# Split weights at five offsets modulo 256 bytes, split activations at another

## The chip, the cores and the metric

The kernel runs on one core of one Trainium2 chip. The metric is the device time of the program in microseconds; before the change it is 2554.64 us, the median of three runs (2552.96 to 2555.19).

## The reference, cut to what matters

Two transformer blocks run one after the other on 256 tokens of width 1024, all in float32. The first has two layers with a feed-forward network, a token mixer and a second feed-forward network, over 256 latent tokens and 256 context tokens. The second has three branches (dilated attention, a short convolution, attention on a memory), gates, and a mixture of 32 experts.

```python
def _swiglu(h, w1, w3, w2):
    return (jax.nn.silu(h @ w1) * (h @ w3)) @ w2
...
    for l in range(DEPTH):
        lat = lat + 0.5 * ml[2] * _swiglu(_modulate(lat, ...), *ffn1)
        cx = cx + 0.5 * mc[2] * _swiglu(_modulate(cx, ...), *ffn1)
        ...
        out_lat, _, _ = _token_mixer(_modulate(lat, ...), *mix_w, s_f, s_b)
        lat = lat + ml[5] * out_lat
        ...
# second block
        merged = (gates[:, :, 0] * (o_attn @ w_proj_attn[l])
                  + gates[:, :, 1] * (z_conv @ w_proj_conv[l])
                  + gates[:, :, 2] * (o_mem @ w_proj_mem[l]))
        x = x + merged @ w_out[l]
        x = x + _hierarchical_moe(h2, ...)   # top 2 of 8 experts of the best of 4 groups
```

The change touches no arithmetic. What matters is that nearly every product before the experts is a float32 matrix product with a weight matrix that is used once.

## The kernel before

All weights of the two blocks but the experts come as units of 128 partitions by 2048 floats (1 MB), in the order in which they are used. `Stream` brings them in: `issue` starts the transfer of a unit into one of three slots `raw`, and `pump` splits each half of it (1024 columns) in two. ScalarE writes the rounded part `wh` in the format fp32r (line 313), VectorE the rest `wl = raw - wh` (line 314). There are five pairs of such tiles (`NSPLIT`), each in a pool of its own (`pst0` to `pst4`), used in turn. A split pair is 8 weight tiles of 128 by 128, or 2 of 128 by 512.

The activations are split the same way: `xh`, `xl` hold the normalised input of a layer (8 tiles of 128 features by 512 tokens), `hh`, `hl` the hidden values of the feed-forward networks, `om` and `mgh`, `mgl` smaller ones of the second block. `mm3` (lines 402 to 404) makes a product of three matmuls: `wl` with `xh`, `wh` with `xl`, `wh` with `xh`. The weights are the stationary operand, which a separate weight load puts in place, the activations the moving one. `wide` (lines 971 to 973) does it the other way round, with the weights moving, 512 columns at a time. With latent and context tokens together a moving operand has 512 columns, with one of them 256. In the profile `p` is the output of the first two feed-forward products, `po` that of output projections, `pz` that of input projections.

Other matrix products (the scan of the mixer, attention, the experts) take plain float32 operands. The experts' weights come as 192 units of 1 MB (`moe_issue`) into whatever tile is free: `moe` in the three raw slots, `ring`, `moex`, `moeom`, `moemgl`, `moexh`, `moexl` and `X`. Expert weights are the moving operand there (lines 1729 and 1757).

The transfers of weights are all issued on the SyncE queue, in the order of the units. The order of the work on each engine follows from the code's order; the `Threads` object interleaves the mixer's scan with the matmuls by a clock of its own.

Tiles are placed by pools that grow from the left or from the right end of a partition's memory. Two fillers set the offsets: `edge` (line 425, 8 floats) on the left ahead of `xh` and `xl`, and `rim` (line 477, 56 floats) on the right after the raw slots, ahead of all pools that follow. `t2` tiles, the scan's `M`, `Q`, `AB` and other left-hand tiles lie after `edge` as well. In the built program the addresses of the main tiles in a partition are, in bytes and modulo 256:

| tile | address before | modulo 256 | address after | modulo 256 |
|---|---|---|---|---|
| X | 16512 | 128 | 16512 | 128 |
| xh, xl (later moexh, moexl) | 33024, 49408 | 0 | 32992, 49376 | 224 |
| hh, hl | 130816, 147200 | 0 | the same | 0 |
| wh, wl of pair 4 | 163584, 167680 | 0 | the same | 0 |
| wh, wl of pair 3 | 171776, 175872 | 0 | 171808, 175904 | 32 |
| wh, wl of pair 2 | 179968, 184064 | 0 | 180064, 184160 | 96 |
| wh, wl of pair 1 | 188160, 192256 | 0 | 188320, 192416 | 160 |
| wh, wl of pair 0 | 196352, 200448 | 0 | 196576, 200672 | 224 |
| raw slots (later moe) | 204544, 212736, 220928 | 0 | 204768, 212960, 221152 | 224 |
| t2 tiles (G, sT, ffa and others) | 76704 and on | 160 | 76672 and on | 128 |
| junk, sc of the modulation | 114208, 95264 | 32 | 114176, 95232 | 0 |
| mgh, mgl, moeom, moemgl | 89440, 154976 | 96 | 89408, 154944 | 64 |
| ring, moex | 97632, 163168 and on | 96 | 97600, 163136 and on | 64 |
| ht, xg of the experts | 188160, 196352 | 0 | 188384, 196576 | 224 |

Every slice that a matmul reads of `wh`, `wl`, `xh`, `xl`, `hh`, `hl`, `mgh` or `mgl` starts a multiple of 512 bytes into its tile, so it has its tile's offset modulo 256.

Of the kernel before, what the change touches and what calls it, by code (L numbers as in the profile page):

```python
# [9 lines left out]
F = mybir.dt.float32  # L10
# [163 lines left out]
R2_QN, R2_KN, R2_QM, R2_KM, R2_B, NR2 = 0, 64, 128, 256, 384, 420  # L174
SUB = 32
OWN = 7
EDGE = (8, 56)


def level_masks():  # L180
# [194 lines left out]
class Kernel:  # L375
# [34 lines left out]
    def run(self):  # L410
        tc, nc, a, es = self.tc, self.nc, self.a, self.es
        self.pc = es.enter_context(tc.tile_pool(name="pc", bufs=1))
        self.pw = es.enter_context(tc.tile_pool(name="pw", bufs=1))
        self.prw, _ = self.pool("prw", "right")
        self.pst = [self.pool("pst%d" % i, "right") for i in range(NSPLIT)]
        self.pf, self.pf_end = self.pool("pf", "right")
        self.pm, self.pm_end = self.pool("pm")
        self.ps = es.enter_context(tc.tile_pool(name="ps", bufs=1, space=PSUM))
        pc = self.pc
        self.S = Stream(self, self.units, a["ws"])  # L420
        self.th = Threads()
        self.X = pc.tile([128, 8, 512], F, name="X")
        self.eps = pc.tile([128, 1], F, name="eps")
        self.lbc = pc.tile([128, 2, 2, 4], F, name="lbc")
        self.edge = pc.tile([128, EDGE[0]], F, name="edge")
        self.operands()
        self.cols = pc.tile([128, NCOL], F, name="cols")
        self.cst = pc.tile([128, NCST], F, name="cst")
        load = nc.sync.dma_start
        load(self.cols, a["cols"])  # L430
        load(self.cst, a["cst"])
        self.post = self.pm.tile([128, 512], F, name="post", tag="AB", bufs=4)[:, :256 + 4 * (T // 64)]
        load(self.post, a["post"])
        load(self.X[:, :, 0:256], a["xin"][:, :, 0:256])
        load(self.X[:, :, 256:512], a["xin"][:, :, 256:512])
        for u in range(NADA):
            load(self.ada_raw[u], a["ws"][u])
            if u in (1, 3):
                self.S.issue(NADA + (u + 1) // 2)
        self.S.issue(NADA + NRAW)  # L440
        self.msk = self.pm.tile([128, 5, 128], I32, name="msk")
        nc.sync.dma_start(self.msk, a["msk"])
        self.ident = self.cst[:, CST_ID:CST_ID + 128]
        self.ones = self.cst[:, CST_ONE:CST_ONE + 128]
        self.sel = self.cst[:, CST_SEL:CST_SEL + 2]
        nc.gpsimd.memset(self.eps, EPS)
        self.scp = pc.tile([128, 8, 36], F, name="scp", tag="scp")[:, :, 0:32]
        nc.gpsimd.memset(self.scp, 0.0)
        nc.scalar.activation(self.scp[:, :, 0:2], self.col("c", "p (a b) -> p a b", b=2), AF.Silu)
        self.lower_bounds()  # L450
        self.spread()
        self.mods = [pc.tile([128, 72, 2], F, name=f"mods{l}") for l in range(2)]
        self.stat_tiles()
        self.AB = {}
        self.first()
        self.second()
        self.moe()
# [16 lines left out]
    def operands(self):  # L474

        self.ada_tiles()
        self.prw.tile([128, EDGE[1]], F, name="rim")

    def ada_tiles(self):

# [1373 lines left out]
```

## Time and profile before

| what | value |
|---|---|
| median of three runs | 2554.64 us |
| profiled execution | 2556.33 us, span 2554.5 us |
| TensorE busy | 2399.6 us, 94% of the span, 14237 matmuls |
| weight loads busy | 1921.3 us, 75% |
| VectorE busy | 1401.8 us, 55% |
| ScalarE busy | 933.7 us, 37% |
| GpSimd busy | 96.4 us, 4% |
| mean granted clock of TensorE | 0.959 |
| read from memory | 510.01 MB, 200 GB/s over the span |

Matmuls are pipelined: each is shown from its start to a modelled end, and overlaps the next. Their rate is read from the distance of starts, or from how many fit in a stretch. A weight load overlaps the matmul before it. In the rows, `out<-in` gives the tiles' names without buffer numbers; of a matmul the moving operand and the stationary one are both inputs.

### The profile page before, as it was taken

To read this page: it belongs to the slowest core of one execution; us is meant where nothing else is said; L and a number is where in the kernel's file an instruction comes from. 1 tells how busy PE (TensorE), PEld (TensorE's weight loads), DVE (VectorE), ACT (ScalarE), POOL (GpSimd) and SP (SyncE) were. 2 spreads that over 40 slices of the span, in tenths; PEclk is the share of its full clock that TensorE was granted. 3 is DMA by queue.
4 is the path that set the end of the run, shared out by engine and by line. 5 is a ranking of instruction groups with operands and counts; after the bars stand their busy time and mean duration, and the time that the engine had idled before them with its cause. 6 is when DMAs were issued, how large, how long until landed. Compare 5 with 4: busy or idle time off the path is not lost.

```text
span 2554.5 us, 34811 instructions
## 1 busy us (share of the span) xinstructions
PE 2399.6 (94%) x14237; PEld 1921.3 (75%) x14237; DVE 1401.8 (55%) x2458; ACT 933.7 (37%) x1481; POOL 96.4 (4%) x125
## 2 busy tenths in 40 slices
PE   7999999999999999999999989999999999776766
PEld 6888888888988888988888879999888984221211
DVE  5777745776787634887534686655776651000000
ACT  5322234676432223422224576545645641000000
POOL 2000001000100001000001010001000000000000
PEclk8999999999999999999999999999999999878877
DMA  7455532112365422455322324555543779999998
GB/s 294 172 191 198 187 126 95 67 50 100 134 229 198 165 99 112 152 210 192 138 89 97 128 73 147 182 182 182 194 144 121 275 285 407 417 415 417 414 417 343
DMA packets 91399, 513.40 MB, mean 201 GB/s; under 512 B 8208, under 2 KB 31264, under 8 KB 32096
## 3 DMA queue, kind: packets, MB, share of 16 engines
q1 hardware_dynamic: 90096, 508.29, 52.4%
q8 instruction: 114, 1.87, 0.3%
q0 software_dynamic: 560, 1.87, 0.2%
q10 hardware_dynamic: 576, 0.94, 0.1%
q14 instruction: 53, 0.43, 0.1%
HBM read 510.01 MB, written 1.05 MB: 200 GB/s over the span
## 4 chain that ended last, share of the span: by engine, by line
PE 44%; DMA 11%; DVE 2%; ACT 1%; SPq 1%; issue 1%; POOL 0%; DVEq 0%; ACTq 0%
PE p L402 5%; PE p L404 5%; PE p L403 5%; DMA ring<-wm 4%; PE po L403 3%; PE po L402 3%; PE po L404 3%; PE pz L402 3%; PE pz L403 3%; PE pz L404 3%; DMA moe<-wm 2%; DMA moex<-wm 2%; DMA moexh<-wm 2%; PE my L1757 2%; PE wide L973 1%; PE wide L971 1%
## 5 line engine op out<-in xcount | busy, mean ns | idle before, releaser
L314 DVE TENSOR_TENSOR wl<-raw,wh 128x1024 fp32r<-128x1024 f32 x428 | 526.7, 1232 | 339.6 <-ACT wh L313 336.1
L313 ACT ACTIVATE wh<-raw 128x1024 fp32r<-128x1024 f32 x428 | 451.6, 1057 | 604.0 <-PE po L404 247.8
L402 PE MATMUL p<-xh,wl 128*128 128x512 f32 (+1 forms) x1608 | 554.5, 347 | 2.0 <-ACT xh L612 2.0
L403 PE MATMUL p<-xl,wh 128*128 128x512 f32 (+1 forms) x1608 | 555.5, 346 | 0.4 <-DVE xl L613 0.4
L404 PE MATMUL p<-xh,wh 128*128 128x512 f32 (+1 forms) x1608 | 555.0, 346 | 0.0
L402 PEld LDWEIGHTS p<-xh,wl 128*128 128x128 f32 x1608 | 303.8, 190 | 41.0 <-ACT xh L612 2.9
L403 PEld LDWEIGHTS p<-xl,wh 128*128 128x128 f32 x1608 | 304.9, 190 | 38.6 <-DVE xl L613 1.1
L404 PEld LDWEIGHTS p<-xh,wh 128*128 128x128 f32 x1608 | 305.0, 190 | 37.0
L512 DVE SCALAR_TENSOR_TENSOR junk<-raw,sc 128x1024 f32<-128x1024 f32 x256 | 304.1, 1234 | 19.1 <-DMA raw<-ws 13.4
L403 PE MATMUL po<-hl,wh 128*128 128x512 f32 (+1 forms) x767 | 266.5, 348 | 0.1
L402 PE MATMUL po<-hh,wl 128*128 128x512 f32 (+1 forms) x767 | 266.4, 348 | 0.0
L404 PE MATMUL po<-hh,wh 128*128 128x512 f32 (+1 forms) x767 | 266.2, 347 | 0.0
L402 PE MATMUL pz<-xh,wl 128*128 128x256 f32 (+1 forms) x672 | 223.7, 333 | 0.0
L403 PE MATMUL pz<-xl,wh 128*128 128x256 f32 (+1 forms) x672 | 211.9, 315 | 0.0
L404 PE MATMUL pz<-xh,wh 128*128 128x256 f32 (+1 forms) x672 | 211.7, 315 | 0.0
L403 PEld LDWEIGHTS po<-hl,wh 128*128 128x128 f32 x767 | 145.2, 189 | 19.1 <-DVE hl L730 0.7
L404 PEld LDWEIGHTS po<-hh,wh 128*128 128x128 f32 x767 | 145.2, 189 | 18.1
L402 PEld LDWEIGHTS po<-hh,wl 128*128 128x128 f32 x767 | 145.0, 189 | 18.3
L727 ACT ACTIVATE ffa<-p 128x512 f32<-128x512 f32 (+1 forms) x88 | 47.9, 544 | 249.2 <-PE p L404 249.2
L402 PEld LDWEIGHTS pz<-xh,wl 128*128 128x128 f32 x672 | 128.4, 191 | 11.6 <-issue 6.2
L404 PEld LDWEIGHTS pz<-xh,wh 128*128 128x128 f32 x672 | 128.3, 191 | 7.5 <-issue 0.2
L403 PEld LDWEIGHTS pz<-xl,wh 128*128 128x128 f32 x672 | 128.6, 191 | 5.7 <-issue 0.5
(424 smaller groups left out, 2908.8 us busy)
## 6 DMA issues: line engine op xcount, KB each, us to landing
raw<-ws SPq DMA_DIRECT2D x279, 1024.0 KB, 4.8
ring<-wm SPq DMA_DIRECT2D x66, 1024.0 KB, 15.4
moe<-wm SPq DMA_DIRECT2D x27, 1024.0 KB, 13.1
moex<-wm SPq DMA_DIRECT2D x27, 1024.0 KB, 16.9
moexh<-wm SPq DMA_DIRECT2D x18, 1024.0 KB, 19.7
moexl<-wm SPq DMA_DIRECT2D x18, 1024.0 KB, 19.7
X<-wm SPq DMA_DIRECT2D x18, 1024.0 KB, 20.2
moeom<-wm SPq DMA_DIRECT2D x9, 1024.0 KB, 20.1
```

The source lines that it names most:

```text
L313: k.nc.scalar.activation(wh, raw, AF.Copy)
L314: k.nc.vector.tensor_sub(wl, raw, wh.bitcast(F))
L402: mm(out, wl, xh, start=start, stop=False, **kw)
L403: mm(out, wh, xl, start=False, stop=False, **kw)
L404: mm(out, wh, xh, start=False, stop=stop, **kw)
L512: v.scalar_tensor_tensor(junk, raw[:, i * 1024:i * 1024 + 1024], 1.0, self.sc[:, p], op0=OP.mult, op1=OP.mult, accum_out=m[:, t + i, p:p + 1])
L727: nc.scalar.activation(t, p1, AF.Silu)
L971: mm(q[n], self.xl[:, kc, ts], wh, start=kc == 0, stop=False)
L973: mm(q[n], self.xh[:, kc, ts], wh, start=False, stop=kc == 7)
L1757: mm(py[32 * j:32 * j + 32, :], hT[:, c * 128 + 32 * j:c * 128 + 32 * j + 32], w[:, c % 2 * 4 + j], start=c == 0, stop=c == 3, skip_group_ ...
```

## The change

The filler `edge` goes, and the filler `rim` goes from the raw slots' pool to the pools of the split weights: 16, 16, 16 and 8 floats (64, 64, 64 and 32 bytes) in `pst0` to `pst3`, none in `pst4`. The sum of the fillers on the right is 56 floats as before, so `hh` and `hl` stay where they were. All engines issue the same instructions in the same order with the same waits; the addresses are as in the table above.

```diff
-EDGE = (8, 56)
+STEP = (16, 16, 16, 8, 0)
...
         self.lbc = pc.tile([128, 2, 2, 4], F, name="lbc")
-        self.edge = pc.tile([128, EDGE[0]], F, name="edge")
         self.operands()
...
         self.ada_tiles()
-        self.prw.tile([128, EDGE[1]], F, name="rim")
+        for (p, _), n in zip(self.pst, STEP):
+            if n > 0:
+                p.tile([128, n], F, name="rim")
```

## Rows read from the trace of the kernel before

**Rows 1.** Busy time by stage: us of each engine, granted clock, DMA share, GB/s
```profile
core 0: us, PE busy (x) PEld busy (x) DVE busy (x) ACT busy (x) POOL busy (x), PEclk, DMA share, GB/s
0.00:60.00 60.00, 46.73 (x342) 37.21 (x346) 31.16 (x68) 32.03 (x59) 13.85 (x20) 0.83 0.75 293
60.00:2110.00 2050.00, 2027.83 (x11583) 1774.34 (x11575) 1342.65 (x2329) 876.88 (x1371) 82.53 (x105) 1.00 0.42 154
2110.00:2555.00 445.00, 325.08 (x2324) 109.73 (x2316) 28.03 (x62) 24.80 (x51) 0.00 (x0) 0.81 1.00 405
```

**Rows 2.** Groups by line and form: count, busy us, mean ns, idle before; 512-column matmuls
```profile
L402 PE MATMUL p<-xh,wl 128*128 128x512 f32 x944 | 367.3, 389 | 0.0
...
L402 PE MATMUL po<-hh,wl 128*128 128x512 f32 x465 | 180.9, 389 | 0.0
...
L972 PE MATMUL wide<-wl,xh 128*128 128x512 f32 x224 | 87.4, 390 | 0.0
...
L402 PE MATMUL pz<-xh,wl 128*128 128x512 f32 x184 | 79.3, 431 | 0.0
...
L402 PE MATMUL po<-xh,wl 128*128 128x512 f32 x40 | 15.6, 389 | 0.0
```

**Rows 3.** Busy time by stage, of line 402 alone
```profile
60.00:2110.00 2050.00, 1104.05 (x3241) 613.80 (x3241) 1.00 0.42 154
```

**Rows 4.** Busy time by stage, a stretch of 512-column and one of 256-column matmuls
```profile
700.00:1000.00 300.00, 300.00 (x1325) 248.43 (x1324) 187.21 (x276) 81.56 (x99) 0.00 (x0) 1.00 0.44 162
1036.00:1058.00 22.00, 22.00 (x184) 21.95 (x183) 17.93 (x37) 11.57 (x20) 0.00 (x0) 1.00 0.18 67
```

**Rows 5.** Timeline of TensorE (start us, duration us), five matmuls left out at each dots
```profile
1059.01 0.40 PE L402 MATMUL p<-xh,wl 128*128 128x512 f32 x1
...
1060.40 0.39 PE L402 MATMUL p<-xh,wl 128*128 128x512 f32 x1
...
1061.76 0.39 PE L402 MATMUL p<-xh,wl 128*128 128x512 f32 x1
```

**Rows 6.** Timeline of TensorE, matmuls on mgh and mgl (2 and 17 left out)
```profile
2064.11 0.28 PE L404 MATMUL po<-mgh,wh 128*128 128x256 f32 x1
...
2064.47 0.29 PE L404 MATMUL po<-mgh,wh 128*128 128x256 f32 x1
...
2066.63 0.29 PE L404 MATMUL po<-mgh,wh 128*128 128x256 f32 x1
```

**Rows 7.** Plain fp32 matmuls by line and by tile: duration ns min/median/max, starts
```profile
L1757 PE MATMUL my<-ring,mhT x336: 379/379/634, 2139.4 to 2544.6; 128*32 128x256 f32 x168
...
L1757 PE MATMUL my<-moe,mhT x128: 379/379/634, 2356.3 to 2469.9; 128*32 128x256 f32 x128
...
L1664 PE MATMUL gat<-G,ht x128: 379/379/796, 2101.7 to 2407.7; 128*128 128x256 f32 x128
...
L1766 PE MATMUL xt<-mys,sT x128: 379/379/797, 2134.9 to 2546.4; 128*128 128x256 f32 x128
```

**Rows 8.** VectorE and ScalarE by line and by tile: duration ns min/median/max
```profile
L314 DVE TENSOR_TENSOR wl<-raw,wh x428: 1207/1225/1874, 23.0 to 2074.3; 128x1024 fp32r<-128x1024 f32 x143
...
L512 DVE SCALAR_TENSOR_TENSOR junk<-raw,sc x256: 1215/1222/1760, 59.2 to 1228.8; 128x1024 f32<-128x1024 f32 x128
...
L313 ACT ACTIVATE wh<-raw x428: 1040/1060/1087, 21.9 to 2073.2; 128x1024 fp32r<-128x1024 f32 x143
...
L729 ACT ACTIVATE hh<-ffa x88: 399/615/636, 76.4 to 1769.3; 128x512 fp32r<-128x512 f32 x66, 128x256 fp32r<-128x256 f32 x22
...
L1517 ACT ACTIVATE mgh<-X x8: 398/404/420, 2041.5 to 2066.5; 128x256 fp32r<-128x256 f32 x8
```

**Rows 9.** Last line of the tile views of raw, moe and ring: issue to landing
```profile
DMA to landing us min/median/max: 4.6/4.8/18.4
...
DMA to landing us min/median/max: 4.8/13.1/20.2
...
DMA to landing us min/median/max: 4.9/15.4/21.5
```

## The prediction

> **What bounds the kernel now.** I read the table of stages first [rows 1]. The span of 2554.5 us has three parts. In the first 60 us TensorE waits for loads. From 60 to 2110 us TensorE is busy for 2027.83 of 2050 us at a granted clock of 1.00 (the 2.4 GHz level), VectorE for 1342.65 and ScalarE for 876.88, the DMA engines for 0.42. From 2110 us on the DMA engines are busy all the time (1.00, 405 GB/s) and TensorE waits for expert weights. So the matmul rate sets the middle, the transfer rate sets the tail, and the splitting engines set next to nothing: the time in which TensorE stands still in the middle is 2050 - 2028 = 22 us.
>
> Then the groups by line and form, and the starts of single matmuls. Nearly all of the middle is triples of split matmuls: 3241 starts on line 402 there [rows 3], as many on 403 and 404, and the 224 wide triples of lines 971 to 973. The 512-column ones are 944 + 465 + 184 + 40 + 224 = 1857 triples [rows 2], 5571 matmuls; the rest of line 402, 3241 - 1633 = 1608 triples, 4824 matmuls, has 256 columns (1633 is the 1857 without the 224 wide ones). Together 10,395. In a stretch with nothing but 512-column ones, 1325 of them fill 300.00 us, and in one with nothing but 256-column ones 184 fill 22.00 us [rows 4], which is 226.4 and 119.6 ns each, with a matmul at each edge counted too often. The starts give it without that error: 1060.40 to 1061.76 us is six spacings of 226.7 ns [rows 5], and the 256-column ones come at 120.0 ns (below). The two differ by 106.7 ns for 256 columns, 0.417 ns a column, which is the 2.4 GHz level; on top of its columns each matmul costs the same 13.3 ns at both widths. TensorE already runs back to back, so an effect of addresses has to show in this 13.3 ns, in the column rate, or not at all.
>
> **What the change does.** It adds and removes no instruction, no wait and no transfer, and the order on every engine stays as it is. It moves bytes. Split activations (xh, xl) go from offset 0 modulo 256 to 224; the five pairs of split weights from 0 to 224, 160, 96, 32 and 0; the raw weight slots from 0 to 224; the hidden activations (hh, hl) stay at 0; nearly all other tiles on the left side go 32 bytes down. So every term is a duration at one offset against the same duration at another, and the trace of before holds tiles at several offsets already.
>
> **Moving operand of a split matmul, off the 256-byte grid.** The output projection of the second block streams mgh and mgl, which lie at offset 96, over weights at 0. The 21 spacings from 2064.11 to 2066.63 us take 2.52 us, 120.0 ns each [rows 6]: equal to the 120 ns of the aligned form. The durations of single ones differ by a few ns in turn (0.28 and 0.29 us), the sum does not. Term: 0 for the 256-column matmuls. For 512 columns no split matmul of before streams from another offset, so I bound it. Below: the 13.3 ns. Above: the only 512-column matmuls that come slower are those just after a change of width, 1059.01 to 1060.40 us, six spacings of 231.7 ns [rows 5], 5.0 ns over the settled rate. I take 0, since the same operand at 256 columns is the nearest row.
>
> **Stationary operand off the grid.** No split matmul of before shows it. The plain fp32 matmuls do: gat loads ht (offset 0), xt loads sT (offset 160), both 128 by 128 against 256 columns, and both take 379 ns in the least and in the median [rows 7]. Their moving side agrees: my streams expert weights from ring (96) and from moe (0), with 379 ns in the least and the median for both [rows 7]. But an fp32 matmul makes several slow passes, so a small cost could be hidden there. I take 0 and keep the bounds of the paragraph above.
>
> **VectorE and ScalarE.** The weight split on VectorE has all three tiles at 0, least 1207 and median 1225 ns; the modulation product of the same size has raw at 0 but junk and sc at 32, and takes 1215 and 1222 ns [rows 8]. ScalarE's split of 1024 elements has a median of 1060 ns at offset 0; at 256 elements the merged activations, 128 to 96, take 404 ns [rows 8]. Between its splits of 512 elements (615 ns) and of 1024, both written at offset 0, ScalarE's slope is (1060 - 615) / 512 = 0.87 ns an element [rows 8]; 404 + 768 x 0.87 = 1072 would be the 1024-element time on the line of the off-grid one, 12 ns from what it is. So offsets cost nothing there, and 22 us of standing TensorE is all that could move. Below and above: a tenth of that, 2 us either way. A split pair lasts 24 matmuls, 24 x 226.7 = 5441 ns, against 1225 on VectorE and 1060 on ScalarE; that is the cover, and it would take a doubling of both to break it even at 120 ns (2880 ns).
>
> **DMA.** In the tail 27 + 18 + 18 of the 192 expert tiles (moe, moexh, moexl) go from 0 to 224, 111 go from 96 to 64 (ring, moex, moeom, moemgl), 18 stay at 128. The quickest landing was 4.6 us for raw and 4.8 for moe (both at 0), and 4.9 for ring (96) [rows 9]; these lie within what a queue does to a transfer, and I take 0. Above: 0.1 of 4.8 us on the 63 moved tiles of 192 in a 445 us tail, 445 x 0.021 x 0.33 = 3 us; below: the same on the other 111, -1 to -5 us were they as slow as that now.
>
> The Trainium skill speaks against the change here: by "DMA: Bandwidth & Descriptors", section "How a descriptor splits into AXI transactions", a transfer that does not start on a 256-byte address begins with a transaction from the boundary below, and the unused bytes cost beats. Were that so for SBUF destinations, by estimate an 8 KB row would have 256 beats at offset 0, 258 at 64, 259 at 96 and 263 at 224, and the tail would lengthen by (63 x 7 - 111 x 1) / (192 x 258) x 445 = 3 us. The quickest landings neither show nor exclude 3 beats in 256, and the sum with this rule would be 2558.
>
> **Sum.** 0 + 0 + 0 + 0. The profiled execution took 2556.33 us (1.8 us around its span of 2554.5), which is 1.7 over the median of the runs, 2554.64 (2552.96 to 2555.19). I forecast 2555 us, with 2549 to 2560 as this case's own range.
>
> **Rivals.**
> First, slower: wide split matmuls off the grid never settle. At a change of width the spacing is 231.7 instead of 226.7 ns for six matmuls and then locks [rows 5]; every operand is on one grid there. With activations at 224 and weights at five offsets the lock might not come. Price: 5.0 ns on the 4176 that read xh or xl (all but the 1395 of po from hh), 21 us, 2576; with those too, whose weights move in four of five pairs, 28 us, 2583. It decides from 0.9 ns a matmul on (5571 x 0.9 = 5 us). For it: those are the only slow matmuls of the stage, and in the offset rows the single durations lose their regularity [rows 6]. Against it: there the mean stays 120.0.
> Second, faster: the 13.3 ns are two streams, next weights and moving columns, that start at one offset and meet. Spread offsets would part them. Price: all of it 10,395 x 13.3 = 138 us, 2417; it counts from 0.5 ns a matmul on. Against it: mgh at 96 over weights at 0 is parted already and still pays 120.0 ns [rows 6].
> Third, the change reaches time only through the tail or the split engines: +3 or -2 us, which cannot be told from the forecast.
>
> **How the numbers follow.** This kernel's runs tell a change from none at about 0.2%, 5 us. Forecast with the third rival: 0.57. First rival, whole or in part: 0.32. Second, nearly always in part: 0.11. The time is the forecast's. The range 2548 to 2574 leaves out the upper part of the first rival (0.12) and most of the second (0.07). Faster 0.11, same 0.57, slower 0.32.
>
> **What the profile after would show.** Right: 512-column split matmuls at 226.7 ns and 256-column ones at 120.0 in the long stretches, whichever pair is in turn; VectorE and ScalarE splits at 1225 and 1060 ns; the tail at 405 GB/s. Wrong towards slower: spacings of 228 ns or more that repeat with the five pairs, with TensorE still busy throughout and the middle part longer by their sum. Wrong towards faster: spacings under 226 ns. If the middle keeps its length and the tail does not, it was the transfers.

## The result and the profile after

The changed kernel takes 2575.77 us (median of four runs, 2573.98 to 2577.23) against 2554.91 of the kernel before on the same chip (2552.96 to 2557.16): a ratio of 1.0081, interval 1.0064 to 1.0098. It is slower by 21 us. The forecast of 2555 was wrong, and the time lies 1.8 us above the range. Its size is that of the first rival (2576), but only part of that rival's mechanism.

The table by stage of the changed kernel, columns as in [rows 1], and below the dots two stretches that answer [rows 4]:

```profile
0.00:60.00 60.00, 46.09 (x346) 37.38 (x350) 31.79 (x68) 32.03 (x59) 13.85 (x20) 0.89 0.75 293
60.00:2130.00 2070.00, 2047.18 (x11607) 1767.85 (x11599) 1343.34 (x2330) 877.04 (x1371) 82.73 (x105) 1.00 0.42 153
2130.00:2575.00 445.00, 316.79 (x2296) 106.29 (x2292) 27.54 (x61) 24.84 (x51) 0.00 (x0) 0.81 1.00 402
...
700.00:1000.00 300.00, 300.00 (x1306) 244.05 (x1306) 190.24 (x282) 79.75 (x96) 0.00 (x0) 1.00 0.44 165
1050.00:1072.00 22.00, 22.00 (x187) 21.95 (x186) 17.98 (x36) 11.33 (x20) 0.00 (x0) 1.00 0.18 66
```

The middle is 20 us longer and TensorE is busy for 19.35 us more in it (2047.18 against 2027.83), at the same granted clock of 1.00; it stands still as little as before (22.8 against 22.2 us). VectorE and ScalarE do the same work in the same time. So nothing waits more: the matmuls themselves come slower. In 300 us there are 1306 of 512 columns instead of 1325. In 22 us there are 187 of 256 columns instead of 184: these come *quicker*. The tail moves 402 GB/s instead of 405.

The groups by line and form, which answer [rows 2], then two 256-column groups and the weight split of [rows 8]:

```profile
L402 PE MATMUL p<-xh,wl 128*128 128x512 f32 x944 | 371.4, 393 | 0.0
L402 PE MATMUL po<-hh,wl 128*128 128x512 f32 x465 | 183.5, 395 | 0.0
L973 PE MATMUL wide<-wl,xh 128*128 128x512 f32 x224 | 88.2, 394 | 0.0
L402 PE MATMUL pz<-xh,wl 128*128 128x512 f32 x184 | 79.4, 432 | 0.0
...
L402 PE MATMUL p<-xh,wl 128*128 128x256 f32 x664 | 185.9, 284 | 2.7 <-ACT xh L613 2.5
L402 PE MATMUL pz<-xh,wl 128*128 128x256 f32 x488 | 143.5, 294 | 0.0
L314 DVE TENSOR_TENSOR wl<-raw,wh 128x1024 fp32r<-128x1024 f32 x428 | 526.0, 1230 | 343.6 <-ACT wh L313 339.8 <-PE tr L1300 2.3
```

Among 512 columns p goes from 389 to 393 ns, po (which reads hh) to 395, wide from 390 to 394. A matmul's duration overlaps the next one, so the spacing of starts says more. The timeline of TensorE at a place where the weights change from the pair at 224 to the pair at 0, with the activations at 224 throughout (17 and 18 matmuls left out at the first and last dots, 4 in the middle):

```profile
82.92 0.39 PE L403 MATMUL p<-xl,wh 128*128 128x512 f32 x1
...
87.00 0.39 PE L403 MATMUL p<-xl,wh 128*128 128x512 f32 x1
...
88.16 0.40 PE L402 MATMUL p<-xh,wl 128*128 128x512 f32 x1
...
92.59 0.40 PE L403 MATMUL p<-xl,wh 128*128 128x512 f32 x1
```

Eighteen spacings in 4.08 us are 226.7 ns, as before, although neither operand is on the 256-byte grid. Nineteen in 4.43 us are 233.2 ns, although the weights are *on* the grid. What differs is whether the two operands lie at the same offset.

Both traces hold the same 10,605 split matmuls in the same order, so I could subtract one kernel's start-to-start times from the other's, one by one:

| term | us |
|---|---|
| first split matmul starts later | +0.8 |
| 512-column matmuls in running chains | +24.0 (reading xh, xl +13.7; hh, hl +8.0; wide +2.3) |
| 256-column matmuls in running chains | -8.5 |
| gaps between chains | -0.2 |
| from the last split matmul to the span's end | +3.9 (462.8 to 466.7) |
| sum | +20.0, the two spans' difference (2574.5 - 2554.5) |

### The profile page after: what moved, and what is told of

It reads as the page before. It is cut to its first block, busy times and chain, and to the rows that moved or that the text cites. A ratio compares the mean times of both kernels' runs of the same rounds, so it can differ in the third digit from the quotient of the medians.

```text
span 2574.5 us, 34811 instructions
## 1 busy us (share of the span) xinstructions
PE 2410.1 (94%) x14237; PEld 1911.5 (74%) x14237; DVE 1402.7 (54%) x2458; ACT 933.9 (36%) x1481; POOL 96.6 (4%) x125
## 4 chain that ended last, share of the span: by engine, by line
PE 43%; DMA 12%; DVE 2%; ACT 1%; SPq 1%; issue 1%; POOL 0%; DVEq 0%; ACTq 0%
PE p L402 5%; PE p L403 5%; PE p L404 5%; DMA ring<-wm 4%; PE po L403 3%; PE po L404 3%; PE po L402 3%; PE pz L402 3%; PE pz L403 3%; PE pz L404 3%; DMA moex<-wm 2%; DMA moexh<-wm 2%; DMA X<-wm 2%; PE wide L974 1%; PE wide L972 1%; PE wide L973 1%
## 5 line engine op out<-in xcount | busy, mean ns | idle before, releaser
L314 DVE TENSOR_TENSOR wl<-raw,wh 128x1024 fp32r<-128x1024 f32 x428 | 526.0, 1230 | 343.6 <-ACT wh L313 339.8
L513 DVE SCALAR_TENSOR_TENSOR junk<-raw,sc 128x1024 f32<-128x1024 f32 x256 | 303.8, 1230 | 18.2 <-DMA raw<-ws 12.5
```

The source lines that it names most:

```text
L314: k.nc.vector.tensor_sub(wl, raw, wh.bitcast(F))
L513: v.scalar_tensor_tensor(junk, raw[:, i * 1024:i * 1024 + 1024], 1.0, self.sc[:, p], op0=OP.mult, op1=OP.mult, accum_out=m[:, t + i, p:p + 1])
```

## The experiments

My theory from this point on: what counts is the *difference* of the two operands' offsets modulo 256 bytes ("relative"). Its rivals: each operand's own distance from the grid ("grid"); the change of offset from one weight pair to the next.

**All operands at one offset off the grid.** Weights, x, h and raw all at 224, no fillers. Against the changed kernel:

```
-STEP = (16, 16, 16, 8, 0)
+STEP = (0, 0, 0, 0, 0)
```

> No fillers at all: split weights, split activations, hidden activations and raw slots all lie at 224 modulo 256, ring, moex and om at 64. Relative theory (only the stationary operand's offset minus the moving one's counts): all differences are 0, so 512-column split matmuls settle at 226.7 ns and 256-column ones at 120.0; the middle is as before, the tail as after the change (about 4 us longer than before): 2559 us. Grid theory (each operand off a multiple of 256 pays): all pay, at least the 25 us of the changed kernel: 2576 to 2590. Change theory (what hurts is that the offset changes from pair to pair): 2555 to 2559, as the relative one.

Measured: 2558.94 us, ratio to before 1.0016 (1.0006 to 1.0025). The two groups that had grown most, in this kernel:

```profile
L402 PE MATMUL p<-xh,wl 128*128 128x512 f32 x944 | 367.3, 389 | 0.0
...
L402 PE MATMUL po<-hh,wl 128*128 128x512 f32 x465 | 180.9, 389 | 0.0
```

Both groups are back at 389 ns with all operands 224 bytes off the grid, and the start-to-start times of all running chains add up to those of before within 0.1 us at either width. The grid theory is out. What remains of the loss sits in the tail: 466.2 us from the last split matmul to the end, as in the changed kernel.

**Only the weights at five offsets** (the raw slots at 224 with them), x and h on the grid:

```
-        self.prw.tile([128, EDGE[1]], F, name="rim")
+        for (p, _), n in zip(self.pst, STEP):
+            if n > 0:
+                p.tile([128, n], F, name="rim")
```

> The five weight offsets as in the change, but xh and xl back at 0 as hh and hl are, and the left-hand tiles as before. Relative theory, with the spacings by difference that the changed kernel shows (0: 227.0, 32: 233.0, 96: 234.3, 160: 233.6, 224: 233.4 ns at 512 columns, 119.8, 118.2, 118.5, 119.9, 116.9 at 256): +5.3 ns on 5571 and -1.2 ns on 5034 matmuls, +29 - 6, and about 2 us in the tail: 2580, above the changed kernel. Grid theory: fewer operands off the grid than in the changed kernel, so below it: 2565 to 2573. Change theory: as the changed kernel, 2576.

Measured: 2581.08 us, ratio 1.0101 (1.0084 to 1.0118).

```profile
L403 PE MATMUL p<-xh,wl 128*128 128x512 f32 x944 | 372.4, 394 | 0.0
...
L403 PE MATMUL po<-hh,wl 128*128 128x512 f32 x465 | 183.5, 395 | 0.0
```

Slower than the changed kernel, though fewer tiles have moved. po on hh pays as it did there, since hh lies at 0 in both. What reads x pays 18.0 us (the wide products 2.9 more) instead of 13.7 and 2.3, and 256 columns give back 6.2 us instead of 8.5. In the changed kernel one unequal pair was cheap: weights at 160 under x at 224 settled at 229 ns, while with x at 0 all four unequal pairs settle at 233 to 234.

**Only the split activations off the grid** (weights and h at 0, left side 32 bytes lower):

```
-        self.edge = pc.tile([128, EDGE[0]], F, name="edge")
```

> Only xh and xl move to 224 (and the left-hand tiles 32 bytes down); all weights, hh, hl and raw at 0. Relative theory: the constant difference 32 on all matmuls that read xh or xl, 233.0 for 226.97 ns on 3504 and 233.4 on 672 of 512 columns (+25 us), 118.2 for 119.8 on some 3840 of 256 columns (-6 us), hh as before, 1 us in the tail: 2575. Grid theory: one of two operands off the grid on 4176 wide matmuls, half the effect or more: 2565 to 2576. Change theory: no change of offset between pairs, so 2555 to 2557.

Measured: 2576.03 us, ratio 1.0078 (1.0062 to 1.0095).

```profile
L402 PE MATMUL p<-xh,wl 128*128 128x512 f32 x944 | 373.4, 396 | 0.0
...
L402 PE MATMUL po<-hh,wl 128*128 128x512 f32 x465 | 181.0, 389 | 0.0
```

Only what reads x pays (396), on all pairs; po on hh stands at 389. The five offsets are not needed for the loss. Split activations 32 bytes lower cost as much as the whole change (+24.6 us at 512 columns, -6.2 at 256), with no change of offset between pairs, so the change theory is out.

**The spacing by itself**, chains of one form without the kernel's other work:

```
PAIRS = [(m, 0) for m in range(0, 256, 16)] + [(4, 0), (8, 0), (128, 128), (224, 224), (32, 96), (192, 0)]
...
                for i in range(NM):
                    ws = s // 4 + 128 * (i % 8)
                    xs = m // 4 + 512 * (i % 4) if n == 512 else m // 4 + 256 * (i % 8)
...
                    nc.tensor.matmul(q[:, 0:n], W[:, ws:ws + 128], X[:, xs:xs + n], start=i == 0, stop=i == NM - 1)
```

> The kernel's work is left out: only chains of 48 fp32r matmuls with a stationary operand at one offset and a moving one at another, 512 and then 256 columns, every 16 bytes of difference and a few pairs with both moved; then 12 transfers of 1 MB to each of six destination offsets, nothing else running. Relative theory: at 512 columns 226.7 ns where the offsets are equal (0 and 0, 128 and 128, 224 and 224) and 229 to 234 where they differ, at 256 columns 120.0 where equal and 116 to 120 where not. Grid theory: 128 and 128, 224 and 224 as slow as 224 over 0. If it needs the other engines' traffic, all are 226.7 and 120.0 here. Transfers: if the destination's offset counts by itself, 0 is the quickest and 224 some 1% to 3% slower; else all the same within 0.5%.

The transfers did not run by themselves, as the text above has it. Nothing made them wait: the last landed at 186 us, so the 512-column chains a to n ran beside them. All later chains, and the two microbenchmarks that follow, ran without any transfer.

The timeline, first matmul of a chain (the letter is the place in the list: a is 0/0, b 16/0, c 32/0, d 48/0, h 112/0, i 128/0, p 240/0, q 4/0; 48 matmuls from one start to the next letter's):

```profile
39.98 0.39 PE L61 MATMUL n512a<-mv,st 128*128 128x512 f32 x1
...
50.86 0.39 PE L61 MATMUL n512b<-mv,st 128*128 128x512 f32 x1
...
61.98 0.40 PE L61 MATMUL n512c<-mv,st 128*128 128x512 f32 x1
...
73.18 0.39 PE L61 MATMUL n512d<-mv,st 128*128 128x512 f32 x1
...
207.21 0.40 PE L61 MATMUL n512p<-mv,st 128*128 128x512 f32 x1
...
218.10 0.40 PE L61 MATMUL n512q<-mv,st 128*128 128x512 f32 x1
...
284.91 0.28 PE L61 MATMUL n256a<-mv,st 128*128 128x256 f32 x1
...
290.67 0.28 PE L61 MATMUL n256b<-mv,st 128*128 128x256 f32 x1
...
324.82 0.28 PE L61 MATMUL n256h<-mv,st 128*128 128x256 f32 x1
...
330.26 0.28 PE L61 MATMUL n256i<-mv,st 128*128 128x256 f32 x1
```

(50.86 - 39.98) / 48 = 226.7 ns at equal offsets; 231.7 for b; (73.18 - 61.98) / 48 = 233.3 for c. At 256 columns 120.0 for a and (330.26 - 324.82) / 48 = 113.3 for h. Settled means of all chains: with equal offsets (0/0, 128/128, 224/224) 226.67 and 119.9 to 120.0. With unequal ones about 229 to 237 at 512 columns, except 240/0 (p: 226.7), and 113.3 to 120.0 at 256, except 4/0 (123.3). No other engine and no stream of loads is needed for it: 192 over 0 takes 233.3 beside the transfers and 233.3 again after their end. The moving operand at 96 over 0 gives 120.0 at 256 columns and 233.3 at 512. The same run wrote 8 KB rows to SBUF by DMA at several offsets; the stretches with offset 0, 32 and 224:

```profile
5.00:30.00 25.00, 19.90 (x76) 16.24 (x77) 0.00 (x0) 4.35 (x3) 0.00 (x0) 1.00 1.01 428
35.00:60.00 25.00, 25.00 (x111) 20.57 (x110) 0.32 (x2) 0.00 (x0) 0.00 (x0) 1.00 1.01 424
...
155.00:180.00 25.00, 25.00 (x109) 20.13 (x108) 0.32 (x2) 0.00 (x0) 0.00 (x0) 1.00 1.01 421
```

On the grid 428 GB/s; off it 424 to 421, with 64, 96 and 128 at 422, 422 and 421. Each offset was run once, 0 first, beside the matmuls. TensorE's start in the first stretch is not the reason: from 15 to 30 us, with TensorE busy throughout, 1 MB landed every 2.45 us, off the grid every 2.48 to 2.50.

**The same difference at other places.**

```
GROUPS = ([(256, a, (a + 64) % 256) for a in (0, 32, 64, 96, 128, 160, 192, 224)] + [(512, 0, 0), (256, 192, 0)]
          + [(256, 32, 96), (256, 192, 0)] + [(512, a, (a + 16) % 256) for a in (0, 64, 128, 176, 240)] + ...
```

> Chains of 96 split matmuls with nothing beside them; the work of the kernel itself is left out. Eight chains of 256 columns have the stationary operand 64 bytes (modulo 256) past the moving one, at eight places. If the difference of the two offsets alone counts, all eight come at one spacing (113 to 118 ns) and the 512-column chains with a difference of 16 all at 226.7 or 231.7 ns. If the distance of an operand from the grid counts, the eight spread over the 113 to 120 ns that single offsets gave, and the ones with an operand at 0 stand apart. If the place in the chain counts (what ran before it), the repeats of moving 192 over stationary 0 differ among themselves.

The timeline, first matmul of a chain of 96 and of the next (g and l: both 256 columns, 192 over 0):

```profile
105.51 0.28 PE L61 MATMUL g256g<-mv,st 128*128 128x256 f32 x1
...
116.82 0.28 PE L61 MATMUL g256h<-mv,st 128*128 128x256 f32 x1
...
172.12 0.28 PE L61 MATMUL g256l<-mv,st 128*128 128x256 f32 x1
...
183.02 0.39 PE L61 MATMUL g512m<-mv,st 128*128 128x512 f32 x1
```

(116.82 - 105.51) / 96 = 117.8 ns for g, (183.02 - 172.12) / 96 = 113.5 for l (settled: 113.3), at the same addresses. The first outcome was what I held likely, and it failed. The eight chains with a difference of 64 gave 117.8 and 113.3 ns in turn; the five 512-column ones with a difference of 16 gave 233.3, 226.7, 226.7, 236.7 and 233.3. Distance from the grid doesn't explain it either: the same addresses (192 over 0) gave 117.8, 117.8 and 113.3. So neither the places nor their difference fixes the rate.

**The same addresses after different predecessors.**

```
PRE = [(512, 0, 0), (256, 0, 0), (128, 0, 0), (384, 0, 0), (512, 64, 64), (512, 128, 0), ...]
GROUPS = [g for p in PRE[:6] for g in (p, (512, 240, 0), p, (512, 0, 0))]
NEXT = [g for p in PRE[:4] for g in (p, (256, 192, 0), p, (256, 0, 0))]
```

> Chains of 48 split matmuls, the kernel's own work left out. The same addresses (512 columns, moving at 240 over stationary at 0; 256 columns, 192 over 0) come after six (four) different predecessors, and beside each the same width with both operands at 0 after the same predecessor. If the offsets fix the spacing, all six are alike and all four are alike. If, with unequal offsets, the spacing is one of several patterns into which the streams fall by what went before, the six lie between 226.7 and 237 ns and the four at 113.3 to 118 without being alike, while the chains with both operands at 0 stand at 226.7 and 120.0 every time.

The timeline, first matmul of each chain (b, f: 240 over 0; z, D: 192 over 0; all others both at 0):

```profile
39.34 0.39 PE L60 MATMUL g512a<-mv,st 128*128 128x512 f32 x1
...
50.22 0.40 PE L60 MATMUL g512b<-mv,st 128*128 128x512 f32 x1
...
61.42 0.39 PE L60 MATMUL g512c<-mv,st 128*128 128x512 f32 x1
...
88.93 0.39 PE L60 MATMUL g512f<-mv,st 128*128 128x512 f32 x1
...
100.28 0.28 PE L60 MATMUL g256g<-mv,st 128*128 128x256 f32 x1
...
288.22 0.28 PE L60 MATMUL g256z<-mv,st 128*128 128x256 f32 x1
...
293.87 0.39 PE L60 MATMUL g512A<-mv,st 128*128 128x512 f32 x1
...
316.26 0.29 PE L60 MATMUL g256D<-mv,st 128*128 128x256 f32 x1
...
321.72 0.28 PE L60 MATMUL g256E<-mv,st 128*128 128x256 f32 x1
```

After a 512-column chain at equal offsets, 240 over 0 takes (61.42 - 50.22) / 48 = 233.3 ns; after a 256-column one (100.28 - 88.93) / 48 = 236.5; in the earlier run the same form took 226.7. At 256 columns z takes 117.7, D 113.8 (settled: 113.3). All six chains of 240 over 0 settled at 233.3 and 236.7 in turn, the four of 192 over 0 at 117.8, 113.3, 113.3 and 113.3. The chains with both operands at 0 settled at 226.67 and 120.00 every time, whatever went before. One more rival has to be looked at: in the built program the three chains of 233.3 write one bank of PSUM (the memory that takes the sums of matmuls) and the three of 236.7 another, so the output tile would explain the six as well as the predecessor does. It does not explain the four, of which the first (117.8) and the third (113.3) write the same bank, and the kernel with x at 240 over 0, two experiments below, rules it out. So the theory has two halves. Equal offsets: one spacing. Unequal offsets: one of a few, and the addresses do not decide which. That what ran before decides it is my reading, and not shown.

**Gain at one width, lose nothing at the other: hidden activations only.** In the last feed-forward stage only 256 columns are read, so hh and hl can lie 48 floats further in their tiles:

```
+        sh = 0 if N == 512 else HOFF          # HOFF = 48 floats = 192 bytes
...
-                post(q[0], q[1], i, slice(lo, hi))
+                post(q[0], q[1], i, slice(lo + sh, hi + sh))
```

> The kernel before with one edit: in the 256-column feed-forward stages the split hidden activations lie 192 bytes off their weights. Relative-offset theory: 906 matmuls of 256 columns at 113.3 instead of 120.0 ns, 6.0 us less, 2549. Grid theory (any operand off the grid costs): 906 at 120.0 or more, 2555 to 2560. A theory in which 256-column matmuls gain only with both operands moved: 2555.

Measured: 2552.14 us, ratio 0.9990 (0.9981 to 0.9999). Those matmuls settle at 114.7 ns on average instead of 119.8. The gain is 2.7 us of matmul time, not 6.0. I had counted 906 matmuls; only 528 belong to that stage, and the other 378 are the 256-column ends of the 512-column stages. 528 x 5.1 = 2.7.

**The same, and x at 240 over weights at 0**, which the first microbenchmark had at 226.7 ns:

```
+    def both(self, name, dt, o=XOFF):         # XOFF = 4 floats; xh and xl as two views of one tile
+        t = self.pc.tile([128, 8192 + EDGE[0]], dt, name=name, tag="xx")
+        return [t[:, o + 4096 * i:o + 4096 * i + 4096] for i in range(2)]
```

> The kernel before with two edits: as in the one above, and the split activations xh, xl at offset 240 over weights at 0. Relative-offset theory, with the spacings of the microbenchmark: 512 columns keep 226.7 ns at 240; 3840 matmuls of 256 columns go from 120.0 to 117.3 (10.4 us less), 906 on the hidden activations from 120.0 to 113.3 (6.0 less), the 672 wide ones whose roles are exchanged from 226.7 to 231 (2.7 more): 13.7 less, 2541. Grid theory: slower than before, 2560 to 2576, as with 224.

Measured: 2567.42 us, ratio 1.0047 (1.0033 to 1.0061), 26 us over what I expected.

```profile
L403 PE MATMUL p<-xx,wl 128*128 128x512 f32 x944 | 374.6, 397 | 0.0
...
L403 PE MATMUL p<-xx,wl 128*128 128x256 f32 x664 | 185.1, 283 | 2.4 <-ACT xx L616 2.3
```

The 256-column terms came (-9.4 us on x, -2.5 on the hidden ones); the 512-column matmuls on x settled at 234.2 ns, not 226.7 (+24.2). The wide ones, priced at 2.7 more, cost nothing (226.7). The cheap 240 of the microbenchmark was one pattern among several. Two stretches of 512-column matmuls on x, at the same two offsets:

```profile
710.00:760.00 50.00, 50.00 (x212) 40.23 (x212) 44.52 (x70) 14.82 (x19) 0.00 (x0) 1.00 0.63 231
820.00:870.00 50.00, 50.00 (x216) 40.19 (x216) 35.96 (x55) 14.07 (x18) 0.00 (x0) 1.00 0.49 180
```

By their starts they come at 236.7 ns in the first and at 233.3 in the second. Each value holds from the start of a stretch to its end, through up to 13 output tiles in a row, and each of the eight PSUM banks of the built program has sums at either value. So the output tile does not decide the spacing. This miss and the repeats above rule out reading a price off a table of offsets.

**What the two halves ask for.** All 512-column operands at one offset (224, no fillers). From the second block's last mixer step on, where x is read by 256 columns only (and by some wide products), both views of x lie 192 bytes further. The larger tile that holds them moves the left-hand tiles 192 bytes up, which puts ring, moex, moeom and moemgl on the 256-byte grid, and one operand of the memory branch is prepared later:

```
+    def xviews(self, o):
+        return [self.xx[:, o + i:o + i + 4096].rearrange("p (m n) -> p m n", m=8) for i in (0, 4096)]
...
+        if l == 1:
+            self.xh, self.xl = self.xviews(HOFF)
```

> All operands of the 512-column matmuls at one offset; from the second block's last mixer step on, where only 256 columns are read, the split activations lie 192 bytes further, as the hidden ones do. 2976 matmuls of 256 columns come with unequal offsets, 336 wide ones of 512 columns too. By the spacings measured at unequal offsets (113.3 to 118.3 against 120.0; wide 229.6 against 226.7): 2976 x (1.7 to 6.7) = 5 to 20 us less, 1 more. Tail: 111 of 192 expert tiles on the 256-byte grid instead of 63; by 3.9 us for 63 tiles that left it, 3 us less. Together 2532 to 2548, likeliest 2540. If an operand off the grid costs by itself: slower than before.

> The same with 64 instead of 192 bytes between activations and weights. If the size of the difference decides: 3 ns less for 192 than for 64 or the reverse, 2976 x 3 = 9 us between the two kernels. If only equal or unequal counts, and the rest is history: both within 3 us.

Measured: 2538.45 us with 192 bytes, ratio 0.9938 (0.9924 to 0.9952); 2543.86 with 64, ratio 0.9960 (0.9946 to 0.9974). The first is 0.6% quicker than the kernel before and by the medians 1.4% quicker than the changed one (2538.45 / 2575.77 = 0.9855). Of the 17.9 us between its profiled span and that of the kernel before, the 256-column matmuls give 16.7 and the tail 2.5; the wide ones cost 0.6 and a later start 1.5, and the gaps between chains give 0.8. Groups of the 192-byte kernel:

```profile
L403 PE MATMUL p<-xx,wl 128*128 128x512 f32 x944 | 367.3, 389 | 0.0
...
L403 PE MATMUL p<-xx,wl 128*128 128x256 f32 x664 | 185.0, 283 | 2.9 <-ACT xx L618 2.9
...
L403 PE MATMUL po<-hh,wl 128*128 128x256 f32 x302 | 84.3, 281 | 0.0
```

512 columns keep 389 ns. The chains of 256 columns with unequal offsets settle at 114.4 ns on average (116.1 with 64 bytes) against 119.8 for those at equal ones. The patterns can be seen to change within one stage, at fixed offsets: the timeline from 1600 us, with 44 and 27 matmuls left out at the first and last dots, and an interruption of TensorE between them:

```profile
1600.03 0.28 PE L403 MATMUL p<-xx,wl 128*128 128x256 f32 x1
...
1605.33 0.28 PE L403 MATMUL p<-xx,wl 128*128 128x256 f32 x1
...
1608.79 0.28 PE L403 MATMUL p<-xx,wl 128*128 128x256 f32 x1
...
1611.96 0.28 PE L404 MATMUL p<-xx,wh 128*128 128x256 f32 x1
```

5.30 / 45 = 117.8 ns ahead of the interruption, 3.17 / 28 = 113.2 after it. The comparison of 192 with 64 bytes stays undecided: the two differ by more than their runs scatter, but 5.4 us lies between the 9 and the 3 that I had set as marks. Both kernels show the same spacings at 256 columns, mixed in other shares.

The seven full kernels and the two compared ones also bear on the tail, with one trace each. Time from the last split matmul to the span's end, by how many of the 192 expert tiles lie on the 256-byte grid: none 466.7 and 466.2 us; 27 463.9; 36 463.4; 63 462.8 (before), 462.2 and 461.3; 111 460.3 and 461.5. More tiles on the grid go with a shorter tail, though 63 and 111 overlap.

## Why the prediction was wrong

- **Reading of the bound: right.** The middle is set by TensorE's rate, its standing still stayed at 22 us, VectorE and ScalarE kept their times (the weight split 1230 ns on average, 1232 before), and the fillers acted through the matmuls and the tail alone.
- **Moving operand off the grid, term 0: wrong. This is the step that failed.** In its place the runs showed 229 to 234 ns instead of 226.7 wherever the changed kernel's two operands lie at unequal offsets at 512 columns, 24.0 us in all. The step took the 256-column row of mgh [rows 6] as the nearest for 512 columns. At 256 columns that difference of offsets happens to give the 120.0 of equal ones; in the microbenchmark, with 96 over 0, 256 columns take 120.0 and 512 columns 233.3. The two widths even have opposite signs: +24.0 us and -8.5 us. The row of the other kind, 231.7 ns after a change of width [rows 5], was closer, and I had it as the upper bound only. The loss of regularity in the single durations at unchanged sum [rows 6] was a sign of another pattern: the starts there come 116 to 125 ns apart in turn, against a settled 120 at equal offsets. I had noted it as an argument for the rival and then let the sum decide.
- **Stationary operand, term 0 from plain fp32 matmuls [rows 7]: wrong.** With the weights alone moved, the time was 2581. The question "this operand or that" was the wrong one as well: both moved together cost nothing in the middle.
- **First rival, 21 us: the size right by luck, the population wrong.** It priced 5.0 ns on all 4176 matmuls that read x. Measured: 16.1 us on those (3.9 ns each, as one pair in five lies at x's own offset and another, at 160, came at 229 ns), 8.0 us on the 1395 that read hh (5.7 ns each), -8.5 us at 256 columns and +3.9 in the tail. These happen to add up to nearly the same. Its larger price, 28 us with those on hh, had the population right (24.0 us measured) and lacked the gain at 256 columns. That they "never settle" is not what the rows show: 233.2 is as steady as 226.7.
- **Second rival, two streams that meet at one offset: refuted as a whole and right in a part.** At 512 columns parting them costs. At 256 columns half of the 13.3 ns can be had (113.3 against 120.0), and the 192-byte kernel has it for most of 2976 matmuls. Whether two streams that meet are the cause is not shown. Its count of 10,395 left out 162 split matmuls before 60 us and 48 wide ones of 256 columns, 3 us of its price.
- **DMA, term 0: too small.** +3.9 us, beyond the upper bound of 3. The quickest landings of single transfers [rows 9] could not show 1%, the bandwidth of a full tail does. The Trainium skill's rule, in "DMA: Bandwidth & Descriptors", section "How a descriptor splits into AXI transactions", was right in direction and, with its 3 us by estimate, near in size. Its proportion of unused bytes is not seen here: 32 bytes off the grid cost 428 to 424 GB/s, 224 bytes 428 to 421. I had let that rule change neither the sum nor a chance. At 421 instead of 428 GB/s the 63 tiles that left the grid, 2.45 us each, lose 2.6 us; where the other 1.3 come from is not shown.
- **The chance.** 0.32 for slower was reasonable for what the rows held; the range ended at 2574 because it cut off the upper part of the first rival.

Still open is why the streams fall into one pattern or another: the traces show starts of matmuls, not reads of SBUF. Nor is it shown what fixes the pattern when a stretch begins: in the kernel with x at 240 over 0, stretches that follow 256-column matmuls ran at 233.3 (from 77 us) and at 236.7 (from 703 us).

## What to carry to other kernels

Where 512-column fp32r matmuls run back to back, give the moving and the stationary tiles the same offset modulo 256 bytes, whichever it is: moving one of them by 32 bytes cost 0.8%. Where 256-column ones do, a difference can gain (here 16.7 us, nearly all of the 0.6%), but measure it in the kernel, since a chain by itself showed one pattern of several. And when the nearest row differs in width from the case, do not let it set the term alone: keep the sign open.

## What was not expected of the hardware

- With equal offsets the spacing settled at one value, whatever ran before: 226.67, 173.33 and 120.00 ns at 512, 384 and 256 columns (the columns at 2.4 GHz and 13.3 ns).
- With unequal offsets it is one of several steady values, which the addresses do not fix: 226.7, 233.3 or 236.7 ns for 240 over 0 at 512 columns, 117.8 or 113.3 for 192 over 0 at 256.
- At 128 columns all chains took 111.7 ns, at equal and at unequal offsets.
- Transfers of 8 KB rows into SBUF that start off the 256-byte grid ran 1 to 1.6% slower (428 to 424 and 421 GB/s), nearly independent of how far off.
